# Memory projections first, the first feed-forward group split by token stream, and modulation weights on a second DMA queue

## The chip, the cores and the metric

The kernel runs on one core of one Trainium2 chip. The metric is the device time of one execution in microseconds, median over runs. The kernel before took 2076.3 us (three runs, 2075.75 to 2080.54).

## The reference, cut to what matters

Two transformer blocks follow each other on 512 latent tokens of width 1024, in float32. Only the first part of the first block is touched by the change:

```
cond_lat = silu(c);  cond_ctx = silu(c_ctx)
m_l = split(cond_lat @ ada_w + ada_b, 9)       # nine modulation vectors, latent tokens
m_c = split(cond_ctx @ ada_w + ada_b, 9)       # the same weights, context tokens
x   = x   + 0.5 * m_l[2] * swiglu(rms_norm(x,   norm1_w) * (1 + m_l[1]) + m_l[0], w1, w3, w2)
ctx = ctx + 0.5 * m_c[2] * swiglu(rms_norm(ctx, norm1_w) * (1 + m_c[1]) + m_c[0], w1, w3, w2)
...                                            # token mixing, a second swiglu
...                                            # second block; its cross attention needs
k = rms_norm(mem) @ w_ck;  v = rms_norm(mem) @ w_cv      # 256 memory tokens
```

x has 512 tokens, ctx and mem have 256 each. The inner width of swiglu is 2816, that is 22 tiles of 128 (f = 0 to 21). Both streams use the same w1, w3 and w2.

## The kernel before, in words

**Numbers.** Each float32 operand of a product is split in two parts of the matmul type, hi and lo. ScalarE makes hi, VectorE makes lo, and three matmuls (hi by hi, hi by lo, lo by hi) make one product. A unit of weights is a 128x1024 tile (512 KB): DMA into `wr`, ScalarE writes `wh`, VectorE writes `wl` (`wload`). A unit is 8 slices of depth, so 24 matmuls of 512 columns for x and 24 of 256 for ctx. `wspare` puts the two parts of a unit into slots of the general pool (`sh`, `sl`) in two halves of 512 columns.

**Buffers.** `wr` has 6 places and is shared by the weights of all products and by the modulation weights (`ada_w`); `wh` and `wl` have `WBUFS` = 5 places each.

**Modulation.** Each of the 9 modulation vectors is made of 8 tiles of `ada_w`, 512 KB each. VectorE multiplies a tile with `cond` and sums along the row, one instruction for each stream (output `junk`, result in a column of `mod`). `ada` does this for vectors 2 to 8, `ada_first` for vectors 0 and 1, inside `first_norm`, one depth slice k after the other.

**Queues.** Every DMA is issued by SyncE (SP), in one order. A load waits at the head of that queue until its place is free, and all loads behind it wait too.

**The planner.** The program writes operations in a program order into `Plan`. `issue()` then replays them with costs (`cost`, `HOPS`, a DMA of SP at 360 bytes a ns plus 50 ns, landing 2000 ns later) and fixes the order of each engine. When an engine is free, the planner takes, among the operations that could start about then, the oldest in program order; VectorE and ScalarE even wait a little for an older one (`YIELD`). On the chip each engine runs its list strictly in order.

**The order at the start.** `cond` and x are loaded, then mem; the first two of six steps of `memory()` come (steps 1 to 4 are one w_ck unit each, 5 and 6 a w_cv pair of units, and the results go to DRAM at the end). `first_norm(lat)` follows: the sum of squares of x, `rsqrt` (12 small VectorE operations), a broadcast (`rb`), and 8 slices k, each with two `ada_first` tiles, `xn`, `hh` and `hl`. As slices come, the first `FIRST` = 7 up-projection units run over them (`begin`), in 7 PSUM banks. Then come the other four steps of `memory()`, and the loads of ctx.

**The first feed-forward part.** `swiglu` takes the 22 tiles in four groups of 6, 6, 5 and 5. In a group, each f needs two up units (w1, w3), then `act` and the split `hi`, `lo`; after the group `project` adds the 8 down units (6 slices, 128x768, in the first group). In the first group (`ahead` = 6) the six f run for x alone, then the same six for ctx with the 12 units loaded again, then the down-projection takes both streams with one load of its weights. `ffn1_side(f)` inserts side steps after each f: two `first_norm(ctx_)` steps for f below 4, four `ada` steps for f = 4 and 5, and three from there on.

Of the kernel before, what the change touches and what calls it, by code (L numbers as in the profile page):

```python
# [11 lines left out]
F32 = mybir.dt.float32  # L12
F32R = mybir.dt.float32r
I32 = mybir.dt.int32
# [17 lines left out]
SLOTS = 60  # L32
WBUFS = 5
TAIL = 3
LEAD = 2

ALONE = 6
FIRST = 7

# [103 lines left out]
class Plan:  # L143
# [8 lines left out]
    PATIENCE = 6000  # L152
    YIELD = 0.3

    def __init__(self, tc):
        self.tc, self.ops, self.caps, self.warm = tc, [], {}, False

# [12 lines left out]
    def add(self, name, engine, method, args, kwargs):  # L170
        outs = [args[0]] + ([kwargs["accum_out"]] if "accum_out" in kwargs else [])
        outs = [x for x in outs if isinstance(x, View)]
        ins = [x for x in list(args[1:]) + [v for k, v in kwargs.items() if k != "accum_out"] if isinstance(x, View)]
        i = len(self.ops)
        deps = set()
        for x in ins:
            deps.update(x.tile.writer[p] for p in x.parts)
        for x in outs:
            for p in x.parts:
                deps.add(x.tile.writer[p])  # L180
                deps.update(x.tile.readers[p])
        for x in ins:
            for p in x.parts:
                x.tile.readers[p].append(i)
        for x in outs:
            for p in x.parts:
                x.tile.writer[p], x.tile.readers[p] = i, []
        deps.discard(None)
        deps.discard(i)
        tiles = {x.tile for x in ins + outs}  # L190
        for t in tiles:
            t.left += 1
            t.last = i
# [6 lines left out]
        self.ops.append((name, engine, method, args, kwargs, deps, tiles, cost, func))  # L200

    def cost(self, name, method, args, kwargs, outs, ins):
# [3 lines left out]
        if name == "PE":  # L206
# [25 lines left out]
    def issue(self):  # L232
# [50 lines left out]
        def pick(e):  # L283
# [26 lines left out]
        while oldest < n:  # L310
# [4 lines left out]
            t0, i = c  # L315
            name, engine, method, args, kwargs, deps, tiles, cost, func = ops[i]
            if func is not None and table not in func:
# [58 lines left out]
def tile_two_blocks(ctx: ExitStack, tc: tile.TileContext, a: dict, out: bass.AP, dbg=None):  # L376
# [128 lines left out]
    def rsqrt(m, cols):  # L505
        y = plan.tile(tp, [P, 32], F32, "rs_y", fresh("rsy"), 2)[:, :cols]
        t = plan.tile(tp, [P, 32], F32, "rs_t", fresh("rst"), 2)[:, :cols]
        V.tensor_scalar(y.bitcast(I32), m.bitcast(I32), 1, None, op0=ALU.logical_shift_right)
        V.tensor_scalar(y.bitcast(I32), y.bitcast(I32), -1, 0x5F3759DF, op0=ALU.mult, op1=ALU.add)
        for _ in range(3):  # L510
            V.tensor_mul(t, y, y)
            V.scalar_tensor_tensor(t, t, -0.5, m, op0=ALU.mult, op1=ALU.mult)
            V.scalar_tensor_tensor(y, t, 1.5, y, op0=ALU.add, op1=ALU.mult)
        return y

    def mean_eps(src, cols, scale):
        m = plan.tile(tp, [P, 32], F32, "rs_m", fresh("rsm"), 2)[:, :cols]
        V.tensor_scalar(m, src, scale, EPS, op0=ALU.mult, op1=ALU.add)
        return m
# [135 lines left out]
    def ada_first(c, s, k, junk):  # L655

        w = wraw(a["ada_w"][c, k], 1024)
        V.tensor_tensor_reduce(junk, w, cond[s], 1.0, col("ada_b", NK * c + k), ALU.mult, ALU.add,
# [106 lines left out]

# [43 lines left out]

    def swiglu(streams, up, down, groups, gate, side=None, after=None, each=None, begun=(), ahead=0):  # L810


        f0, first = 0, ahead
        for g, F in enumerate(groups):
            hid = {st: [] for st in streams}

# [6 lines left out]
            def some(f, part):  # L823
# [10 lines left out]
                ws = [None if ps[i] else wcols(wload(up[2 * f + i])) for i in range(2)]  # L834
                if g == 0 and f < LEAD and not first:
                    for span in spans_of(streams):
# [24 lines left out]
            project(lambda o: wcols(wload(down[g][o], F * P), F), lambda st: hid[st], update, streams,  # L861
                    after if g == len(groups) - 1 else None, each if g == len(groups) - 1 else None)
            f0 += F

    normal = first_norm(ctx_)
    rest = (step for c in range(2, 9) for step in ada(c, (0, 1) if c < 5 else (0,)))

    def ffn1_side(f):
        if f < 4:
            for _ in range(2):  # L870
                next(normal, None)
        else:
            for _ in range(4 if f < 6 else 3):
                next(rest, None)

    swiglu([lat, ctx_], a["ffn1_up"], [a[f"ffn1_dn{g}"] for g in range(len(FFN1_GROUPS))], FFN1_GROUPS,
           per_stream(lambda s: half_gate(2, s)), ffn1_side,
           renorm(per_stream(lambda s: gain_of("norm2_w", 4, s)), per_stream(lambda s: shift_of(3, s))), begun=sums, ahead=ALONE)
    for k in range(NK):
# [872 lines left out]
```

## Time and profile before

| | us |
|---|---|
| median of three runs | 2076.3 |
| profiled execution, its own time | 2077.35 |
| its span, first to last instruction | 2075.5 |
| TensorE busy | 2009.8 |
| VectorE busy | 1190.4 |
| ScalarE busy | 794.5 |

The profiled execution lies 1.05 us over the median and inside the range of the runs. TensorE is busy for 97% of the span, but its busy time also counts matmuls at half clock. PE is TensorE, DVE VectorE, ACT ScalarE, POOL GpSimd and SP SyncE.

### The profile page before, as it was taken

What the parts mean: (1) busy time and instruction counts of PE and PEld (TensorE: products, weight loads), DVE (VectorE), ACT (ScalarE), POOL (GpSimd) and SP (SyncE); (2) the same over time, 40 slices, a digit from 0 to 9 for tenths busy, and PEclk for the clock granted to TensorE, in tenths of its full rate; (3) what the DMA queues carried; (4) which work ended last, traced back from release to release, by engine and by line L of the source; (5) the groups of instructions that cost most, each with busy time, mean ns of one, the idle gap of its engine ahead of it and who ended that gap; (6) DMA issues with size and microseconds to landing.
All of it is one profiled execution on the core that took longest, in us unless ns stands there. A gap on an engine that the chain in (4) does not pass through costs nothing.

```text
span 2075.5 us, 27876 instructions
## 1 busy us (share of the span) xinstructions
PE 2009.8 (97%) x11033; PEld 1688.6 (81%) x11033; DVE 1190.4 (57%) x2157; ACT 794.5 (38%) x1238; POOL 121.1 (6%) x126
## 2 busy tenths in 40 slices
PE   5889999999999998999999999999998999999998
PEld 4779888888888876978988888888765888888887
DVE  7887844426247788589633333374866655343344
ACT  5452121221225654374432222343676363233231
POOL 0000000000000023110000000001243010000000
PEclk9989999999999999999999999999997999999999
DMA  8866624417132112232233323234321214333321
GB/s 312 270 236 199 196 77 140 145 60 224 51 107 94 45 52 72 67 91 83 71 117 101 97 92 104 86 94 124 85 74 27 64 59 132 101 92 102 93 70 41
DMA packets 73538, 225.57 MB, mean 109 GB/s; under 512 B 9360, under 2 KB 12096, under 8 KB 73408
## 3 DMA queue, kind: packets, MB, share of 16 engines
q1 hardware_dynamic: 73408, 223.80, 34.7%
q8 instruction: 86, 1.41, 0.3%
q14 instruction: 44, 0.36, 0.1%
HBM read 210.00 MB, written 5.24 MB: 104 GB/s over the span
## 4 chain that ended last, share of the span: by engine, by line
PE 87%; issue 5%; DVE 3%; DMA 2%; ACT 2%; POOL 1%; SPq 0%; DVEq 0%; ACTq 0%; POOLq 0%
PE p L363 77%; PE as L363 1%; PE gs L363 1%; PE ro L363 1%; PE rs L363 1%; PE at L363 1%; PE ao L363 1%; PE st L363 1%; PE go L363 1%; DVE junk L363 1%; DMA wr<-in_ffn_up_dram 1%; PE gl L363 1%; DVE rg_r L363 0%; PE rb L363 0%; POOL pg L363 0%
## 5 line engine op out<-in xcount | busy, mean ns | idle before, releaser
L363 ACT ACTIVATE wh<-wr 128x1024 fp32r<-128x1024 f32 (+4 forms) x295 | 298.2, 1012 | 751.1 <-PE p L363 566.1
L363 PE MATMUL p<-hh,wh 128*128 128x512 f32 (+1 forms) x1320 | 505.2, 389 | 13.2 <-ACT hh L363 7.9
L363 PE MATMUL p<-hl,wh 128*128 128x512 f32 (+1 forms) x1320 | 507.2, 388 | 0.0
L363 DVE TENSOR_TENSOR wl<-wr,wh 128x1024 fp32r<-128x1024 f32 (+4 forms) x295 | 345.9, 1177 | 170.7 <-ACT wh L363 77.6
L363 PE MATMUL p<-hh,wl 128*128 128x512 f32 (+1 forms) x1320 | 363.4, 387 | 4.3 <-DVE wl L363 4.3
L363 PE MATMUL p<-lo,wh 128*128 128x512 f32 (+1 forms) x831 | 310.0, 381 | 2.5 <-DVE lo L363 2.5
L363 PE MATMUL p<-hi,wh 128*128 128x512 f32 (+1 forms) x831 | 308.7, 380 | 2.0 <-ACT hi L363 2.0
L363 PEld LDWEIGHTS p<-hh,wh 128*128 128x128 f32 x1320 | 248.9, 190 | 57.6 <-ACT hh L363 10.4
L363 PEld LDWEIGHTS p<-hh,wl 128*128 128x128 f32 x1320 | 243.9, 190 | 54.5 <-DVE wl L363 4.7
L363 PEld LDWEIGHTS p<-hl,wh 128*128 128x128 f32 x1320 | 250.9, 191 | 37.5 <-issue 1.3
L363 PE MATMUL p<-hi,wl 128*128 128x512 f32 (+1 forms) x831 | 211.6, 375 | 0.0
L363 PEld LDWEIGHTS p<-lo,wh 128*128 128x128 f32 x831 | 158.6, 191 | 27.4 <-DVE lo L363 3.2
L363 PEld LDWEIGHTS p<-hi,wh 128*128 128x128 f32 x831 | 158.3, 191 | 24.4 <-ACT hi L363 2.2
L363 PEld LDWEIGHTS p<-hi,wl 128*128 128x128 f32 x831 | 148.8, 188 | 27.2
L363 PEld LDWEIGHTS p<-h,wh 128*128 128x128 f32 x816 | 138.8, 189 | 26.1
L363 DVE CUSTOM_DVE_ANT_0 junk<-wr,cond,vec 128x1024 f32<-128x1024 f32 x112 | 143.3, 1281 | 21.0 <-DMA wr<-in_ada_w_dram 20.1
L363 PE MATMUL p<-h,wh 128*128 128x256 f32 x816 | 145.5, 280 | 0.0
L363 DVE TENSOR_TENSOR act<-act,p 128x512 f32<-128x512 f32 (+1 forms) x68 | 38.3, 583 | 176.9 <-PE p L363 175.5
L363 DVE SCALAR_TENSOR_TENSOR x<-p,gate,x 128x512 f32<-128x512 f32 (+1 forms) x59 | 42.6, 723 | 106.0 <-PE p L363 106.0
L363 DVE TENSOR_TENSOR x<-p,x 128x512 f32<-128x512 f32 (+1 forms) x51 | 33.6, 658 | 112.9 <-PE p L363 112.7
L363 PE MATMUL p<-h,wl 128*128 128x256 f32 x408 | 97.3, 279 | 0.0
L363 PEld LDWEIGHTS p<-hid,wh 128*128 128x128 f32 x352 | 64.3, 188 | 14.3
(344 smaller groups left out, 2434.6 us busy)
## 6 DMA issues: line engine op xcount, KB each, us to landing
wr<-in_ffn_up_dram SPq DMA_DIRECT2D x100, 512.0 KB, 3.7
wr<-in_ada_w_dram SPq DMA_DIRECT2D x88, 512.0 KB, 4.4
wr<-in_mlp_up_dram SPq DMA_DIRECT2D x32, 512.0 KB, 3.6
wr<-in_mlp_dn_dram SPq DMA_DIRECT2D x32, 512.0 KB, 3.6
wr<-in_w_out_dram SPq DMA_DIRECT2D x16, 512.0 KB, 4.2
wr<-in_ffn_dn_dram SPq DMA_DIRECT2D x16, 448.0 KB, 3.2
wr<-in_ffn_dn_dram SPq DMA_DIRECT2D x16, 384.0 KB, 3.2
wr<-in_ffn_dn_dram SPq DMA_DIRECT2D x16, 320.0 KB, 2.8
```

The source lines that it names most:

```text
L363: ins = getattr(engine, method)(*args, **kwargs).ins
```

## The change

The memory stream is loaded ahead of x, the first memory step runs ahead of `first_norm(lat)`, and one more memory step follows after each slice. `cond` is loaded after x. The number of units begun early is 6. The first group runs whole for x, down-projection included, then whole for ctx; both its up and its down weights are loaded twice. Three side steps follow each f of each pass; they are now vector 2 for x (8 steps), the load and the first norm of ctx (8), vector 2 for ctx (8), then vectors 3 to 8. The modulation weights get 3 places of their own (`wa`) and are issued by GpSimd; `wr` has 5 places, `wh` and `wl` have 4. The planner treats a DMA of any queue by the cost of SP's, and VectorE takes an operation of `mean_eps` and `rsqrt` ahead of older ones if it can start within 200 ns.

```
-WBUFS = 5
+WBUFS = 4
+RAWS = 5
+ARAWS = 3
...
-ALONE = 6
-FIRST = 7
+FIRST = 6
...
+    RUSH = 200
+    LANDING = 2000
+    def hurry(self):          # a context in which self.urgent is True
...
-        if name == "SP":
+        if method == "dma_start":
             x = outs[0] if outs else ins[0]
             return int(np.prod(x.shape)) * 4 / 360.0 + 50
...
             if e in ("DVE", "ACT"):
+                rush = [c for c in cand if ops[c[1]][9] and c[0] - first <= self.RUSH]
+                if rush:
+                    return min(rush)
...
-            landed = end + (2000 if e == "SP" else 0)
+            landed = end + (self.LANDING if method == "dma_start" else 0)
...
-    def wraw(ap, cols):
-        raw = plan.tile(wp, [P, 1024], F32, "wr", fresh("wr"), 6)
-        sync.dma_start(raw[:, :cols], ap)
+    def wraw(ap, cols, queue=sync, tag="wr", n=RAWS):
+        raw = plan.tile(wp, [P, 1024], F32, tag, fresh(tag), n)
+        queue.dma_start(raw[:, :cols], ap)
         return raw
+
+    def araw(c, j):
+        return wraw(a["ada_w"][c, j], 1024, G, "wa", ARAWS)
...                            # rsqrt and mean_eps: the same operations, inside "with plan.hurry():"
-            w = wraw(a["ada_w"][c, j], 1024)
+            w = araw(c, j)
...                            # the same in ada_first
-    cond = [conditions(0), None]
+    mem = load(NC, "mem", a["memT"])
+    early = memory()
+    next(early)
     lat = load(NL, "x", a["xT"])
     xt = lat.x
-    mem = load(NC, "mem", a["memT"])
-    early = memory()
-    for _ in range(2):
-        next(early)
+    cond = [conditions(0), None]
...
     for k in range(NK):
         next(normal)
+        next(early, None)
...
-    for _ in early:
-        pass
-    ctx_ = load(NC, "ctx", a["ctxT"])
-    cond[1] = conditions(1)
+    ctx_ = Stream(NC, None)
...
-        f0, first = 0, ahead
-        for g, F in enumerate(groups):
-            hid = {st: [] for st in streams}
+        passes = [(0, [st]) for st in streams] if apart else [(0, streams)]
+        passes += [(g, streams) for g in range(1, len(groups))]
+        count = 0
+        for g, part in passes:
+            f0, F = sum(groups[:g]), groups[g]
+            hid = {st: [] for st in part}
...
-                some(f, streams[:1] if f < first else streams)
-                if f == first - 1:
-                    for e in range(first):
-                        some(e, streams[1:])
+                some(f, part)
                 if side is not None:
-                    side(f)
+                    side(count)
+                count += 1
...                            # project(...) takes part instead of streams
+    def second_norm():
+        ctx_.x = load(NC, "ctx", a["ctxT"]).x
+        cond[1] = conditions(1)
+        yield from first_norm(ctx_)
...
+    rest = chain(ada(2, (0,)), second_norm(), ada(2, (1,)),
+                 *(ada(c, (0, 1) if c < 5 else (0,)) for c in range(3, 9)))
+
+    def ffn1_side(i):
+        for _ in range(3):
+            next(rest, None)
```

## Rows read from the trace of the kernel before

**Rows 1.** The page: busy time of each engine, share of the span, instructions.
```profile
PE 2009.8 (97%) x11033; PEld 1688.6 (81%) x11033; DVE 1190.4 (57%) x2157; ACT 794.5 (38%) x1238; POOL 121.1 (6%) x126
```

**Rows 2.** Windows by stage: length, then busy us and instructions of each engine.
```profile
core 0: us, PE busy (x) PEld busy (x) DVE busy (x) ACT busy (x) POOL busy (x), PEclk, DMA share, GB/s
0.00:79.20 79.20, 57.67 (x253) 47.26 (x254) 61.65 (x131) 45.14 (x77) 0.70 (x6) 0.94 0.85 296
79.20:126.80 47.60, 36.40 (x212) 31.84 (x211) 40.20 (x86) 20.08 (x34) 0.00 (x0) 0.86 0.76 243
126.80:226.90 100.10, 100.10 (x643) 90.70 (x642) 81.71 (x123) 32.96 (x43) 0.00 (x0) 1.00 0.67 214
...
600.00:900.00 300.00, 287.94 (x2161) 244.09 (x2160) 213.97 (x440) 146.63 (x266) 48.15 (x56) 0.99 0.24 73
...
1450.00:1700.00 250.00, 239.04 (x1199) 176.44 (x1198) 168.72 (x322) 147.30 (x269) 66.41 (x60) 0.93 0.21 59
1700.00:2075.50 375.50, 365.55 (x1701) 306.19 (x1699) 168.28 (x247) 121.82 (x158) 0.00 (x0) 0.99 0.30 91
```

**Rows 3.** Waits of PE, 0 to 126.8 us: total, times, longest.
```profile
PE st L363 <- DVE ss L363: 13.3, 1, 13.3
PE p L363 <- ACT hh L363: 6.7, 5, 3.8
PE p L363 <- ACT wh L363: 5.3, 3, 2.3
PE p L363 <- DVE wl L363: 4.3, 1, 4.3
PE rb L363 <- DVE rsy L363: 2.9, 1, 2.9
```

**Rows 4.** Timeline of SP's queue: start, length, count, in the first 112 us.
```profile
1.63 4.63 SPq L363 DMA_DIRECT2D x<-in_xT_dram  x8
7.23 2.35 SPq L363 DMA_DIRECT2D mem<-in_memT_dram  x4
...
97.92 12.78 SPq L363 DMA_DIRECT2D wr<-in_ada_w_dram  x4
111.98 1.84 SPq L363 DMA_DIRECT2D wr<-in_ffn_up_dram  x2
```

**Rows 5.** Timeline, ACT and PE: the unit that was loaded late.
```profile
117.22 1.06 ACT L363 ACTIVATE wh<-wr 128x1024 fp32r<-128x1024 f32 x1 [3.67 <-DMA wr<-in_ffn_up_dram]
...
118.33 0.80 PE L363 MATMUL p<-hh,wh 128*128 128x512 f32 x1 [1.80 <-ACT wh L363]
```

**Rows 6.** Timeline of PE at full clock: spacing of matmuls, 512 and 256 columns.
```profile
69.67 0.39 PE L363 MATMUL p<-hh,wh 128*128 128x512 f32 x1
...
78.97 0.39 PE L363 MATMUL p<-hh,sl 128*128 128x512 f32 x1
...
82.07 2.08 PE L363 MATMUL p<-h,sh 128*128 128x256 f32 x16
83.98 1.12 PE L363 MATMUL p<-h,sl 128*128 128x256 f32 x8
```

**Rows 7.** Groups of DVE by form, 0 to 226.9: busy us, mean ns, idle before.
```profile
L363 DVE CUSTOM_DVE_ANT_0 junk<-wr,cond,vec 128x1024 f32<-128x1024 f32 x64 | 81.9, 1280 | 3.9 <-DMA wr<-in_ada_w_dram 3.3
L363 DVE TENSOR_TENSOR wl<-wr,wh 128x1024 fp32r<-128x1024 f32 x26 | 31.1, 1218 | 0.0
L363 DVE TENSOR_TENSOR sl<-wr,sh 128x512 fp32r<-128x512 f32 x20 | 13.3, 688 | 1.6 <-PE p L363 1.0 <-issue 0.5
L363 DVE TENSOR_TENSOR wl<-wr,wh 128x768 fp32r<-128x768 f32 x8 | 7.4, 949 | 0.0
```

**Rows 8.** Timeline of DVE: first and last operation of x's reciprocal root (merged with mem's).
```profile
16.95 0.16 DVE L363 TENSOR_SCALAR rsm<-st 128x4 f32<-128x4 f32 x1 [0.49 <-PE st L363]
...
25.74 0.23 DVE L363 SCALAR_TENSOR_TENSOR rsy<-rst,rsy 128x2 f32<-128x2 f32 x2
```

**Rows 9.** DMA issues: count, KB each, median us to landing; the page, then 10:80.
```profile
wr<-in_ada_w_dram SPq DMA_DIRECT2D x88, 512.0 KB, 4.4
...
wr<-in_ada_w_dram SPq DMA_DIRECT2D x20, 512.0 KB, 5.4
```

More of the change, by code (lines that the diff above doesn't have):

```diff
@@ L153, with __enter__, __exit__ @@
     YIELD = 0.3
+    RUSH = 200
+    LANDING = 2000
     def __init__(self, tc):
-        self.tc, self.ops, self.caps, self.warm = tc, [], {}, False
+        self.tc, self.ops, self.caps, self.warm, self.urgent = tc, [], {}, False, False
+    def hurry(self):
+        plan = self
+        class Hurry:
+            def __enter__(self):
+                plan.urgent = True
+            def __exit__(self, *_):
+                plan.urgent = False
+        return Hurry()
     def engine(self, name, engine):
@@ L199, in add @@
         cost = self.cost(name, method, args, kwargs, outs, ins)
-        self.ops.append((name, engine, method, args, kwargs, deps, tiles, cost, func))
+        self.ops.append((name, engine, method, args, kwargs, deps, tiles, cost, func, self.urgent))
     def cost(self, name, method, args, kwargs, outs, ins):
@@ L315, in issue @@
             t0, i = c
-            name, engine, method, args, kwargs, deps, tiles, cost, func = ops[i]
+            name, engine, method, args, kwargs, deps, tiles, cost, func, _ = ops[i]
             if func is not None and table not in func:
@@ L507, in rsqrt @@
         t = plan.tile(tp, [P, 32], F32, "rs_t", fresh("rst"), 2)[:, :cols]
[L508 to L513, printed above, removed]
+        with plan.hurry():
+            V.tensor_scalar(y.bitcast(I32), m.bitcast(I32), 1, None, op0=ALU.logical_shift_right)
+            V.tensor_scalar(y.bitcast(I32), y.bitcast(I32), -1, 0x5F3759DF, op0=ALU.mult, op1=ALU.add)
+            for _ in range(3):
+                V.tensor_mul(t, y, y)
+                V.scalar_tensor_tensor(t, t, -0.5, m, op0=ALU.mult, op1=ALU.mult)
+                V.scalar_tensor_tensor(y, t, 1.5, y, op0=ALU.add, op1=ALU.mult)
         return y
@@ L517, in mean_eps @@
         m = plan.tile(tp, [P, 32], F32, "rs_m", fresh("rsm"), 2)[:, :cols]
-        V.tensor_scalar(m, src, scale, EPS, op0=ALU.mult, op1=ALU.add)
+        with plan.hurry():
+            V.tensor_scalar(m, src, scale, EPS, op0=ALU.mult, op1=ALU.add)
         return m
@@ L655, in ada_first @@
     def ada_first(c, s, k, junk):
-        w = wraw(a["ada_w"][c, k], 1024)
+        w = araw(c, k)
         V.tensor_tensor_reduce(junk, w, cond[s], 1.0, col("ada_b", NK * c + k), ALU.mult, ALU.add,
@@ L807, in log1p_exp_neg, with swiglu @@
         return s
-    def swiglu(streams, up, down, groups, gate, side=None, after=None, each=None, begun=(), ahead=0):
-        f0, first = 0, ahead
-        for g, F in enumerate(groups):
-            hid = {st: [] for st in streams}
+    def swiglu(streams, up, down, groups, gate, side=None, after=None, each=None, begun=(), apart=False):
+        passes = [(0, [st]) for st in streams] if apart else [(0, streams)]
[4 more added lines that the diff above has]
+            hid = {st: [] for st in part}
             def finish(span, t, hi, lo, p1, p3):
@@ L834, in some @@
                 ws = [None if ps[i] else wcols(wload(up[2 * f + i])) for i in range(2)]
-                if g == 0 and f < LEAD and not first:
+                if g == 0 and f < LEAD and not apart:
                     for span in spans_of(streams):
@@ L859, in update, with chain @@
                 V.scalar_tensor_tensor(st.x[o][:, x:y], po, gate(st)(o), st.x[o][:, x:y], op0=ALU.mult, op1=ALU.add)
-            project(lambda o: wcols(wload(down[g][o], F * P), F), lambda st: hid[st], update, streams,
+            project(lambda o: wcols(wload(down[g][o], F * P), F), lambda st: hid[st], update, part,
                     after if g == len(groups) - 1 else None, each if g == len(groups) - 1 else None)
[L863 to L874, printed above, removed]
+    def second_norm():
+        ctx_.x = load(NC, "ctx", a["ctxT"]).x
+        cond[1] = conditions(1)
+        yield from first_norm(ctx_)
+    def chain(*steps):
+        for s in steps:
+            yield from s
+    rest = chain(ada(2, (0,)), second_norm(), ada(2, (1,)),
+                 *(ada(c, (0, 1) if c < 5 else (0,)) for c in range(3, 9)))
+    def ffn1_side(i):
+        for _ in range(3):
+            next(rest, None)
     swiglu([lat, ctx_], a["ffn1_up"], [a[f"ffn1_dn{g}"] for g in range(len(FFN1_GROUPS))], FFN1_GROUPS,
            per_stream(lambda s: half_gate(2, s)), ffn1_side,
-           renorm(per_stream(lambda s: gain_of("norm2_w", 4, s)), per_stream(lambda s: shift_of(3, s))), begun=sums, ahead=ALONE)
+           renorm(per_stream(lambda s: gain_of("norm2_w", 4, s)), per_stream(lambda s: shift_of(3, s))), begun=sums, apart=True)
     for k in range(NK):
```

## The prediction

> **What bounds the kernel now.** I read the page's busy times first. PE is busy 2009.8 of 2075.5 us [rows 1], so 65.7 us of idle time and whatever the half clock costs is all that can be won. The windows by stage say where they lie [rows 2]: 21.5 us up to 79.2, 11.2 us from there to 126.8, none up to 900 except 12.1 us after 600, and some 21 us in the last two rows. The change edits only the start; the later stages keep their work, so I look at the first 226.9 us, the time at which the first feed-forward group ends.
>
> Idle time is not all that is lost there, since the granted clock is 0.94 and 0.86 in the first two stretches against 1.00 in the third. I count work instead. At full clock 41 matmuls of 512 columns take 9.30 us, 0.227 each, and 16 of 256 columns 1.91 us, 0.119 each [rows 6]. By the code the 253 matmuls of the first stretch are 7 units x 24 = 168 wide ones, 48 of 256 columns (two memory units) and some 36 small ones (0.12 taken for each): 38.1 + 5.7 + 4.3 = 48.1 us of work in 79.2 us, so 31.1 us are lost. The 212 of the second are 144 of memory, 12 small ones and 56 wide: 17.1 + 1.4 + 12.7 = 31.2 us of work, 16.4 us lost. Together 47.5 us are lost, and the whole first group with all that stands ahead of it is 226.9 - 47.5 = 179.4 us of PE work.
>
> The waits name the causes [rows 3]. The 13.3 us are the first bytes: x, then the sum of squares. The ACT hh waits are the slices of x's first norm. The ACT wh and DVE wl waits are units that came late. For those see SP's queue: four modulation loads stand at its head for 12.78 us from 97.92, and the next up units go out at 111.98 [rows 4]. One of them is split at 117.22 and PE restarts at 118.33 [rows 5]. So the loss of the second stretch comes from one shared ring and one shared queue, with VectorE behind them: it frees a place only after its `junk` instruction.
>
> And VectorE is nearly full itself: 61.65 + 40.20 + 81.71 = 183.6 busy us of 226.9 [rows 2], with 64 junks at 1.28 us as the largest item [rows 7].
>
> **The change part by part.**
>
> *Memory first.* x's first DMA goes out at 1.63 us now [rows 4]. Ahead of it come 1 MB of mem and 0.5 MB of w_ck, while 1.5 MB of modulation tiles run on the other queue; at the 296 GB/s of the first row [rows 2] 1.5 to 3 MB are 5 to 10 us. x's statistics are that much later, but PE has a memory unit to do, and the chain of the reciprocal root, 16.95 to 25.97 us now with other work between its 12 operations [rows 8], can run in 12 x 0.2 = 2.4 us once `hurry` puts them first. The two cancel within a few us, and I take nothing for the start of the slices. What counts is that all eight memory units (4 w_ck, 2 pairs of w_cv, 192 matmuls) now fill holes between slices. At the end of the early sums PE has done 144 x 0.227 + 192 x 0.119 + 36 x 0.12 = 59.8 us of work. The slices are set by VectorE, which gets 9 more half-unit splits there at 0.69 us [rows 7] and loses a junk and the seventh unit's split, 2.5 us: +3.7 us. If half of this is hidden in VectorE's own holes, the sums end at 81, and 21 us are lost in place of 31.1: -10.
>
> *Own ring and own queue.* Up units no longer wait behind modulation tiles, and ctx's norm runs beside x's remaining three f and its down-projection, 6 x 24 x 0.227 + 8 x 18 x 0.227 = 65.4 us of PE work. The 16.4 us of the second stretch go. With the term above, PE alone would end the group at 179.4 + 21 = 200.4.
>
> *What VectorE then has to do.* Eight down units of the first group are split once more, 8 x 0.949 = 7.6 us [rows 7]. The side steps now follow 12 passes over f and not 6: by program order 72 junks (16 of x's norm, 8, 16 of ctx's norm, 8, 16, 8) are older than the end of the group, against 64 now: 8 x 1.36 with the read of the sum = 10.9 us. (Vector 2 costs 8 more loads, no more junks: two single ones in place of a pair.) VectorE's work to the end of the group is 183.6 + 7.6 + 10.9 = 202.1 us. Its idle time was 43.3 us. It cannot start before the first bytes, so at least 8 us remain; I take 15, and 25 as the other end. Half of the last side step, some 4 us, may trail behind. That puts the end at 202 + 15 - 4 = 213, between 202 and 227: VectorE, not PE, sets it. The loss comes back in the ctx pass, where an f is 48 x 0.119 = 5.7 us of PE work, but two splits (2.4 us), three steps with up to six junks (8.2 us) and more for VectorE; the planner gives it the oldest first, and that is the junk of the f before, while the unit that PE wants next waits behind it.
>
> *Three places for modulation tiles.* A tile's place turns round in 5.2 us in the planner (0.13 + 1.51 + 2.0 + 0.13 + 1.4). In the trace the load alone takes 4.4 us, and 5.4 where DMA is busy [rows 9], so 6.1 to 7.1 with issue and junk. Where single junks follow each other (32 tiles behind x's norm, 10.7 turns) VectorE can stand 0.9 to 1.9 us a turn, 10 to 20 us in all, if nothing else were planned between; in most turns something is, so 0 to 20 with 4 taken, for this and for a low clock behind the holes. No row shows a DMA issued by GpSimd; I take the landing of SP's for it, from 4.4 us to 5.4 and 2.5 more for the range. The Trainium skill, DMA: Bandwidth & Descriptors, Specifications, gives the GpSimd path a first byte after about 1 us against 0.6 on SP's path; 0.4 us on 10.7 turns would be 4 us, and the sum would be 2071 by it, an estimate. No row here shows it.
>
> *The rest at nothing.* One place less for `wr`, `wh` and `wl` still leaves four units, over 20 us of PE work at 24 x 0.227 = 5.4 us a unit, against some 7 us for load and split; if that cover is gone it shows in the windows from 600 on, 3 us either way. `hurry` later in the kernel moves operations of 0.16 us under a busy PE. The 8 added down loads and 8 added modulation loads, 7 MB, fit into a DMA share of 0.67 to 0.85.
>
> **The sum.** The group ends at 213 + 4 = 217 in place of 226.9: -9.9. From the profiled execution, 2077.35 us, that is 2067.4; it lies 1.05 us over the median, inside the spread of the runs, and I give **2067**. About 0.3%, 6.2 us, is what a measurement of this kernel can tell from no change.
>
> **The rivals.**
>
> *VectorE lags without harm (0.18).* A junk whose tile has not come lets a split go first, so the backlog slides into the next group, where an f of both streams is 16.6 us of PE work. Then PE alone sets the end, 200 to 204: 2050 to 2055. For it: two-thirds of the turns above have a hole for one split. Against it: vectors 3 and 4 have two junks a tile, 2.7 us, and no hole.
>
> *Loss moved, not removed (0.24).* VectorE idles 25 us as it waits for x, cond and late tiles, and the ctx pass starves: end at 221 to 232, 2071 to 2082. For it: VectorE was 0.78 busy in the first stretch even with full rings.
>
> *Modulation tiles land late (0.25).* The order of VectorE is fixed by a planner that believes in 2.0 us and in two queues that do not share bandwidth. If a tile takes 2.5 us more than 4.4, every turn holds the splits behind it: 10.7 x 2.5 = 27 us more, end at 244, 2094. It decides against the change from about 5.9 us of landing on (1.5 x 10.7 = 16 us). For it: 5.4 us already in 10:80 with one queue. Against it: x's slices leave 8 us for three junks. The Trainium skill, SBUF — State Buffer, section SBUF: two separate sides, has a mechanism for it: GpSimd cannot write descriptors while VectorE runs in a two-port mode. The large groups of rows 7 are two-input operations, which by that page hold off only GpSimd operations that read SBUF, so by the rule little is to be feared.
>
> **Chances.** The forecast's own case, 2060 to 2070, has 0.33. Faster by over 0.3%: 0.33 + 0.18 = 0.51. Within: 0.24. Slower: 0.25. The range from 2049 to 2092 takes in the PE-bound case below and most of the late tiles above, and leaves some 0.18 outside.
>
> **What would show it.** In the profile of after: PE's first matmul near 10 us; the sums done near 81; no wait of SP for `mod` ahead of an up load; PE idle in the ctx pass on ACT wh or DVE wl with VectorE at 0.9 or more; the step to continuous 512-and-256 pairs near 217. Wrong if VectorE is below 0.85 in that stretch, if junk waits for DMA exceed 20 us, or if the stages from 600 on move by more than 5 us.

## The result and the profile after

The changed kernel takes 2106.2 us (median of 4 runs, 2099.8 to 2108.3) against 2078.4 beside it (4 runs, 2075.8 to 2081.3): a ratio of 1.0122, 95% interval 1.0094 to 1.0151. A second set of four runs gave 1.0118 (1.0089 to 1.0147). It is slower by 1.2%; 2067 was predicted, and the range ended at 2092. The profiled execution took 2104.78 us, its span is 2103.0, 27.5 more than before.

The page of the changed kernel shows PE 11 us busier, and DVE only by 10 (columns as in [rows 1]):

```profile
PE 2020.9 (96%) x11033; PEld 1696.6 (81%) x11033; DVE 1200.1 (57%) x2165; ACT 803.3 (38%) x1247; POOL 172.9 (8%) x222
```

PE does the same instructions as before; 11 us more of busy time is a lower granted clock (0.976 over the span against 0.981), the other 16 of the 27.5 are idle time. The windows by stage of the changed kernel say where (columns as in [rows 2]; the third window ends where the second group begins, 246.20 here and 226.76 before):

```profile
0.00:79.20 79.20, 54.91 (x307) 48.70 (x308) 57.83 (x121) 44.00 (x78) 9.30 (x22) 0.91 0.88 310
79.20:126.80 47.60, 43.26 (x193) 35.33 (x193) 41.37 (x83) 19.45 (x28) 10.03 (x19) 0.98 0.73 229
126.80:246.20 119.40, 100.78 (x608) 91.16 (x606) 101.25 (x158) 39.93 (x54) 14.77 (x28) 0.91 0.74 247
...
1700.00:2103.00 403.00, 392.31 (x1859) 328.86 (x1857) 182.59 (x291) 140.64 (x211) 7.38 (x13) 0.99 0.28 88
```

The third stretch was full in before, at clock 1.00 [rows 2]; now PE idles 18.6 us in it, at 0.91. With the 179.4 us of PE work that the prediction counted, 246.2 - 179.4 = 66.8 us are lost up to there in place of 47.4: 19.4 of the 27.5 us lie in the first group. DVE is busy 57.83 + 41.37 + 101.25 = 200.5 us in it and idle for 45.7: 21.4 us up to 79.2, 6.2 from there to 126.8, and 18.1 behind. What PE waited for there, 0 to 246.2 us (total, times, longest):

```profile
PE p L383 <- DVE wl L383: 21.5, 6, 7.0
PE p L383 <- ACT sh L383: 17.2, 3, 13.3
PE rb L383 <- DVE rsy L383: 2.5, 1, 2.5
PE st L383 <- DVE ss L383: 2.2, 1, 2.2
```

The ACT hh and ACT wh waits of [rows 3] have almost gone; DVE wl, a unit whose low half is not split, has become the largest. The timeline of PE shows these holes: two in the passes of the latent tokens, two in those of the context, and the second group's first matmul at the end.

```profile
125.60 5.40 PE L383 MATMUL p<-hh,wl 128*128 128x512 f32 x16 [4.12 <-DVE wl L383]
142.52 5.45 PE L383 MATMUL p<-hh,wl 128*128 128x512 f32 x16 [6.97 <-DVE wl L383]
...
219.31 2.08 PE L383 MATMUL p<-h,wl 128*128 128x256 f32 x8 [4.44 <-DVE wl L383]
231.93 1.65 PE L383 MATMUL p<-hid,wl 128*128 128x256 f32 x6 [4.38 <-DVE wl L383]
...
246.20 0.40 PE L383 MATMUL p<-hh,wh 128*128 128x512 f32 x1
```

And this is VectorE ahead of the hole at 219.31:

```profile
211.09 0.42 DVE L383 TENSOR_TENSOR act<-act,p 128x256 f32<-128x256 f32 x1 [0.41 <-PE p L383]
211.43 1.28 DVE L383 CUSTOM_DVE_ANT_0 junk<-wa,cond,vec 128x1024 f32<-128x1024 f32 x1
...
212.64 0.42 DVE L383 TENSOR_TENSOR hid<-act,hid 128x256 fp32r<-128x256 f32 x1
212.98 1.28 DVE L383 CUSTOM_DVE_ANT_0 junk<-wa,cond,vec 128x1024 f32<-128x1024 f32 x1
...
214.30 1.28 DVE L383 CUSTOM_DVE_ANT_0 junk<-wa,cond,vec 128x1024 f32<-128x1024 f32 x1
...
215.51 1.28 DVE L383 CUSTOM_DVE_ANT_0 junk<-wa,cond,vec 128x1024 f32<-128x1024 f32 x1
...
216.83 1.28 DVE L383 CUSTOM_DVE_ANT_0 junk<-wa,cond,vec 128x1024 f32<-128x1024 f32 x1
...
218.04 2.36 DVE L383 TENSOR_TENSOR wl<-wr,wh 128x1024 fp32r<-128x1024 f32 x2
220.31 1.28 DVE L383 CUSTOM_DVE_ANT_0 junk<-wa,cond,vec 128x1024 f32<-128x1024 f32 x1
...
223.85 0.42 DVE L383 TENSOR_TENSOR act<-act,p 128x256 f32<-128x256 f32 x1 [2.25 <-PE p L383]
```

Five junks run with one short operation between them, none waits for its tile, and only then come the two splits. PE, idle for 4.44 us, starts when the first of them is done, and then VectorE waits 2.25 us for PE's result. The two engines take turns. Of VectorE's 18.1 idle us behind 126.8, its waits for PE make up 12.7 us; the two largest are:

```profile
DVE act L383 <- PE p L383: 10.0, 7, 2.3
DVE ctx L383 <- PE p L383: 2.4, 3, 1.4
```

ScalarE stands behind the same splits, since wh and wl have four places each:

```profile
219.34 0.84 ACT L383 ACTIVATE wh<-wr 128x768 fp32r<-128x768 f32 x1 [6.09 <-DVE wl L383]
```

The start is late as well. The eight slices of x's norm, by DVE's operation on tile xn (first and last start), ran from 29.9 to 69.1 in before; in the changed kernel:

```profile
L383 DVE TENSOR_TENSOR xn<-x,rbs x8: 684/687/693, 34.2 to 83.2; 128x512 f32<-128x512 f32 x8
```

That is 4.3 us later, and 7.0 us a slice in place of 5.6. The early sums end at 94.0.

### The profile page after: what moved, and what is told of

The parts are those of the page before. It is cut to its first block, busy times and chain, and to the rows that moved or that the text cites. A ratio compares the mean times of both kernels' runs of the same rounds, so it can differ in the third digit from the quotient of the medians.

```text
span 2103.0 us, 27943 instructions
## 1 busy us (share of the span) xinstructions
PE 2020.9 (96%) x11033; PEld 1696.6 (81%) x11033; DVE 1200.1 (57%) x2165; ACT 803.3 (38%) x1247; POOL 172.9 (8%) x222
## 4 chain that ended last, share of the span: by engine, by line
PE 84%; issue 5%; DVE 5%; DMA 2%; ACT 2%; POOL 1%; SPq 0%; DVEq 0%; POOLq 0%; ACTq 0%
PE p L383 75%; PE as L383 1%; PE gs L383 1%; DMA wr<-in_ffn_up_dram 1%; PE ro L383 1%; PE st L383 1%; DVE junk L383 1%; PE rs L383 1%; PE go L383 1%; PE at L383 1%; PE ao L383 1%; PE gl L383 1%; PE rb L383 0%; DMA wr<-in_w_ck_dram 0%; DMA wa<-in_ada_w_dram 0%
## 5 line engine op out<-in xcount | busy, mean ns | idle before, releaser
L383 ACT ACTIVATE wh<-wr 128x1024 fp32r<-128x1024 f32 (+4 forms) x303 | 305.0, 1008 | 731.2 <-PE p L383 521.6
L383 DVE TENSOR_TENSOR wl<-wr,wh 128x1024 fp32r<-128x1024 f32 (+4 forms) x303 | 355.0, 1175 | 158.9 <-ACT wh L383 78.9
L383 PE MATMUL p<-hi,wl 128*128 128x512 f32 (+1 forms) x831 | 206.1, 374 | 0.0
L383 PEld LDWEIGHTS p<-hi,wl 128*128 128x128 f32 x831 | 148.7, 188 | 27.5 <-DVE wl L383 0.3
L383 DVE CUSTOM_DVE_ANT_0 junk<-wa,cond,vec 128x1024 f32<-128x1024 f32 x112 | 143.1, 1281 | 13.5 <-DMA wa<-in_ada_w_dram 12.1
L383 PEld LDWEIGHTS p<-h,wl 128*128 128x128 f32 x408 | 71.2, 194 | 6.3 <-DVE wl L383 6.2
```

The lines of the kernel that those rows point to most:

```text
L383: ins = getattr(engine, method)(*args, **kwargs).ins
```

## The experiments

Sixteen runs followed, e15 and e16 of the two kernels themselves. Of each are given the ratio to before with its 95% interval; the **group end**, the first matmul of the second group in the trace (226.8 in before, 246.2 in the changed kernel); and, where it helps, the **time at equal clock**: span times mean granted clock over 0.981, the mean over the runs. Spans of before lie up to 19 us apart, and with them the mean clock (0.976 to 0.987); their product lies between 2072 and 2082 in single runs, and its mean hardly moves. In four sets of 24 to 31 runs before comes to 2076.4, 2076.9, 2076.8 and 2076.6. PE's work being the same, this number follows PE's idle time: 65.7 us over the whole span in before, and 82.1 in the changed kernel, which comes to 2094.2. The group end is that of one profile each; two profiles of before put it at 226.8 and 224.1, so a difference below 3 us in it says little.

**Does VectorE's order starve PE, or its amount of work?** e1 takes steps out of the context's pass, e2 changes the order alone: it marks the splits of the first group's units with `hurry`, so that the planner gives them ahead of older operations.

```diff
 def ffn1_side(i):
-    for _ in range(3):
+    for _ in range(1 if 6 <= i < 12 else 3):
         next(rest, None)
```

> The changed kernel with one modulation step instead of three behind each of the six f of the context pass; the 12 steps left out there follow in the later groups, so nothing is left out of the computation. Theory A (VectorE works off modulation tiles that are older in the program than the splits TensorE waits for): 24 junks x 1.36 = 33 us of VectorE work leave a pass that took some 71 us for 51 us of TensorE work; the context pass loses most of its 20 us, the first group ends at 228 to 235 instead of 247, and the time is 2087 to 2094. Theory B (the up and down units themselves come late over the DMA, VectorE only waits with them): within 3 us of the changed kernel's 2106. Theory C (the junks only move their stall into the next group): the first group ends earlier, but the stage up to 670 gives it back and the time stays above 2100.

Measured: 1.0033 (1.0008 to 1.0057), group end 230.5. Both numbers of A came, 2089.3 us being 17 less than the changed kernel. B and C fall: the junks cost little where they went (2080.8 at equal clock against 2094.2).

```diff
+    def rushed(ap, cols):      # wload, for the first group's units
+        ...
+        with plan.hurry():
+            split(hi[:, :cols], lo[:, :cols], raw[:, :cols])
```

> The changed kernel, with the splits of the first group's up and down units marked like the reciprocal root, so that the planner gives them ahead of older junks; the work is the same. Theory A (order): TensorE gets its units in time, the junks slide behind; the first group ends at 230 to 237, 2089 to 2096. Theory D (amount: VectorE has too much to do before the group's end, whatever the order, since the outputs of an f need it too): gain below 4 us, 2102 to 2108.

Measured: 1.0011 (0.9983 to 1.0040), 2081.9 us, group end 227.3. With the same work in another order the first group ends 18.9 us earlier, and in the median the loss against before is no longer measurable; at equal clock (2080.9) some 4.5 us of it are left. That is more than A expected; D falls. Not all of the 18.9 us is idle time won: up to its group end VectorE is busy 187.7 us here, 12.8 less than in the changed kernel, and idle for 39.6, 6.1 less. e6 marks the outputs of each f too.

```diff
+                with plan.hurry() if apart and g == 0 else ExitStack():
                     S_.activation(t[:, x:y], p1, AF.Silu)
                     V.tensor_mul(t[:, x:y], t[:, x:y], p3)
                     split(hi, lo, t[:, x:y])
```

> As e2_split_first, and the three output operations of each f of the first group marked too, so that every junk yields to what TensorE waits for. In e2 one wait of 10.2 us for an output (hi) was left in the latent pass. Theory A: that wait goes and the first group ends 6 to 10 us earlier than e2's 227.3, at 217 to 221; the time 2070 to 2078, 4 to 10 us below e2. Theory D (the wait only moves, to the gate's tiles or to context's norm, which the junks feed): the group ends within 3 us of 227.3 and the time stays within 4 us of e2.

Measured: 1.0026 (1.0004 to 1.0049), group end 217.2. The end is as A expected, the median is not: it is 2080.1, within 4 us of e2, as D had it. At equal clock e6 comes to 2076.6, 4.3 below e2, so part of what the group won is there. In the two profiles the rest took 1857.7 us in e6 and 1849.6 in e2, which is for the most part the clock (see e15). VectorE in the context's pass of e6:

```profile
182.95 0.42 DVE L383 TENSOR_TENSOR act<-act,p 128x256 f32<-128x256 f32 x1 [0.34 <-PE p L383]
183.29 1.22 DVE L383 TENSOR_TENSOR wl<-wr,wh 128x1024 fp32r<-128x1024 f32 x1
184.43 0.42 DVE L383 TENSOR_TENSOR hid<-act,hid 128x256 fp32r<-128x256 f32 x1
184.76 1.28 DVE L383 CUSTOM_DVE_ANT_0 junk<-wa,cond,vec 128x1024 f32<-128x1024 f32 x1
...
185.97 1.22 DVE L383 TENSOR_TENSOR wl<-wr,wh 128x1024 fp32r<-128x1024 f32 x1
187.11 1.28 DVE L383 CUSTOM_DVE_ANT_0 junk<-wa,cond,vec 128x1024 f32<-128x1024 f32 x1
```

One junk stands between two splits, not five. Up to the group's end VectorE is busy 178.2 us here against 200.5: the junks that nobody waits for slide into the next groups (58 start before the end, 72 in the changed kernel). The windows up to the group end, e2 and then e6 (columns as in [rows 2]):

```profile
0.00:227.33 227.33, 189.58 (x1104) 168.32 (x1105) 187.69 (x340) 103.49 (x161) 32.24 (x66) 0.95 0.81 277
0.00:217.24 217.24, 188.52 (x1104) 168.35 (x1105) 178.22 (x326) 104.19 (x161) 30.02 (x61) 0.97 0.83 281
```

**The start.** e3 gives the head the order of before; e7 gives SP the tiles of x's norm as well; e8 does two memory units ahead of the slices and six behind them.

```diff
+    cond = [conditions(0), None]
+    lat = load(NL, "x", a["xT"])
     mem = load(NC, "mem", a["memT"])
     early = memory()
     next(early)
-    lat = load(NL, "x", a["xT"])
-    cond = [conditions(0), None]
```

> The changed kernel with the three loads at its head in the order of the kernel before: conditions, x, then memory. Theory S (x and the conditions stand behind 1.5 MB of memory and the modulation tiles, and every slice of x's norm is late by that): x's reciprocal root ends near 20 instead of 29.7, the sums end at 82 to 87 instead of 93, and the time is 6 to 11 us less, 2095 to 2100. Theory T (the slices are set by VectorE's amount of work with the memory splits, not by their start): the sums end within 3 us of 93 and the time stays within 3 us of 2106.

Measured: 1.0126 (1.0090 to 1.0162), group end 246.2, slices from 35.8 to 84.1. T, the slices starting even later than without the edit. The order at the head is worth nothing while a second queue loads tiles beside it. From issue to landing, in the first 42 us (count, KB each, median us), before:

```profile
x<-in_xT_dram SPq DMA_DIRECT2D x8, 256.0 KB, 6.1
```

and the changed kernel:

```profile
wa<-in_ada_w_dram POOLq DMA_DIRECT2D x7, 512.0 KB, 5.7
x<-in_xT_dram SPq DMA_DIRECT2D x8, 256.0 KB, 9.0
```

The Trainium skill, DMA: Bandwidth & Descriptors, Rules for kernel authors, says that issuing from several engines wins no bandwidth, since all run on the same 16 DMA engines and interleave. The trace agrees: x's pieces take half as long again (9.6 us in e3, where they go out first) while tiles land beside them of which the changed kernel uses none before 24 us.

```diff
-        w = araw(c, k)
+        w = wraw(a["ada_w"][c, k], 1024, sync if s == 0 else G, "wa", ARAWS)
```

> As e6_outputs_too, with conditions and x loaded first as in the kernel before, and the modulation tiles of x's own norm issued by SP behind x (own ring kept); all later tiles stay with GpSimd. Theory Q (with a second queue 1.5 MB of tiles land beside x from the first microsecond and take its bandwidth: x's loads took 9.6 to 10.3 us against 6.1, whichever order stood at the head): x's first slice starts near 30 instead of 35 and the time is 3 to 7 us below e6. Rival T (the slices are paced by VectorE and ScalarE work, not by their start): the last slice stays within 2 us of 85, and the time within 2 us of e6.

Measured: 1.0036 (1.0014 to 1.0058), group end 224.1, first slice at 36.5. The edit does not test Q. GpSimd's queue still sends three tiles, of later vectors now, at the very start:

```profile
1.29 0.72 POOL L383 DMA_DIRECT2D wa<-in_ada_w_dram  x1 [0.35 <-issue]
...
2.35 1.09 POOL L383 DMA_DIRECT2D wa<-in_ada_w_dram  x2
```

So 1.5 MB land beside x as before, and x's loads still took 9.6 us. T falls: the last slice starts at 65.0, 18.6 us earlier than in e6, and yet the group ends 6.8 us later and the median is 5.7 us longer. PE's first matmul came at 20.9 us (13.8 in e6); whether that is the reason no run shows.

```diff
     early = memory()
-    next(early)
+    for _ in range(2):
+        next(early)
 ...
         next(normal)
-        next(early, None)
 ...
+    for _ in early:
+        pass
     ctx_ = Stream(NC, None)
```

> As e6_outputs_too, with two memory units ahead of the slices and the other six behind them, as in the kernel before. Theory M (the nine half-unit splits between the slices stretch them from 5.6 to 7.1 us each): the slices end near 74 instead of 85; what is won there is spent on the memory units behind, which TensorE then has in one piece, so the group ends between 4 us earlier and 6 us later than in e6. Theory P (the memory units fill holes that are there anyway): the group ends 6 to 12 us later and the time is as much above e6.

Measured: 1.0001 (0.9978 to 1.0023), group end 217.0, slices in e8:

```profile
L383 DVE TENSOR_TENSOR xn<-x,rbs x8: 685/689/693, 36.3 to 73.0; 128x512 f32<-128x512 f32 x8
```

5.2 us a slice in place of 7.0, and the same end: M, near its middle. The memory units stretch the slices as much as they save behind them, so "memory first" is worth nothing at the group end in either direction (2074.4 at equal clock, 2 us below e6).

**Ring and queue.** e4 puts only the own ring and GpSimd's queue into before. e10 takes both out of the changed kernel. e12 and e13 do the same with the marks of e6 and the memory order of e8: own ring on SP's queue, and shared ring.

```diff
-WBUFS = 5
+WBUFS = 4
...
-        raw = plan.tile(wp, [P, 1024], F32, "wr", fresh("wr"), 6)
+    def araw(c, j):
+        return wraw(a["ada_w"][c, j], 1024, G, "wa", 3)      # other loads: "wr", 5
```

> The kernel before with only the own ring and GpSimd's queue for modulation tiles, and the one place less for each of the three unit rings that pays for it; the order of the first group and of its start stays. As the prediction put it (the shared ring and queue cost 16.4 us between 79.2 and 126.8): 8 to 16 us less than before's 2078, 2062 to 2070. Rival R2 (tiles on that queue land late, with VectorE's fixed order behind them): 2085 to 2095. Rival V (VectorE takes the place of the ring: the same junks stand ahead of the same splits): within 5 us of 2078.

Measured: 1.0031 (1.0010 to 1.0051), 2084.1 us, group end 232.1. The queue and ring that were to win 16 us lose 5 at the group end, and 11 at equal clock (2087.8). V names part of it: PE's idle time from 79.2 to 126.8 falls from 11.2 to 3.1 us, as the prediction had it, and 9.2 us of it come behind, where before had none. The time lies 1 us beyond V's range, since the start is worse as well: x's pieces took 10.3 us to land, the first slice began at 38.9, and PE idled 30.0 us up to 79.2 in place of 21.5. R2 is out: behind the first tile, junks waited 3.6 us for their tiles.

```diff
-        return wraw(a["ada_w"][c, j], 1024, G, "wa", ARAWS)
+        return wraw(a["ada_w"][c, j], 1024)
```

(and the places of before, 6 raw and 5 split)

> The changed kernel with modulation tiles back on SP's queue and in the shared ring, and the places of before (6 raw, 5 split); memory first, the first group apart, the three steps an f and the marks on the root stay. Theory A (the loss is made by VectorE's order, whatever the queue): the first group ends at 238 to 250, the time is 2092 to 2106. Theory Q (the second queue, or the places given up for it, makes the loss): the group ends at 220 to 230, 2068 to 2082.

Measured: 1.0073 (1.0045 to 1.0101), group end 240.0. A by the end, its time missed by 1 us: without own ring and queue the loss stays, though smaller (2087.3 at equal clock).

```diff
-        return wraw(a["ada_w"][c, j], 1024, G, "wa", ARAWS)
+        return wraw(a["ada_w"][c, j], 1024, sync, "wa", ARAWS)
```

> As e8_memory_last, with the tiles issued by SP again but in their own ring of three. Theory Q2 (own queue: a tile that waits for its place no longer holds the units behind it on SP): without it the first group ends at 222 to 232 instead of 217, and the time is 5 to 15 us above e8. Rival N (the ring is what matters, or nothing does): the group ends within 3 us of 217 and the time within 4 us of e8.

Measured: 0.9961 (0.9940 to 0.9982), 2068.1 us, group end 212.8. Both theories fall: taking GpSimd's queue away is a gain, 4.2 us of the group (the ratio's interval just overlaps that of e8). x's pieces land in 7.7 us (9.7 in e8), the first slice starts at 33.7 (36.3), and PE idles 20.7 us up to 79.2 (25.1), so the gain lies at the start. This version beats both kernels.

e13 has e10's edit on top of e8's kernel, with e10's places.

> As e12_tiles_on_sp, but with the shared ring and the places of before (6 raw, 5 split): what is left of the change is the first group apart, the context's norm beside it and the marks. Ring theory (tiles and units that share six places hold each other up even when VectorE gives the units first): the first group ends at 218 to 228 instead of 212.8, and span times clock over 0.981 is 2074 or more, against 2068.3 for e12. Rival (one queue, in the right order, is enough): within 3 us of e12 in both.

Measured: 1.0059 (1.0036 to 1.0083), group end 237.6, 2082.4 at equal clock. The ring theory, and more: 24.8 us. SP's queue in e13 shows it (start, length, count):

```profile
94.64 10.90 SPq L383 DMA_DIRECT2D wr<-in_ada_w_dram  x6
106.75 4.95 SPq L383 DMA_DIRECT2D wr<-in_ffn_up_dram  x2
116.64 7.99 SPq L383 DMA_DIRECT2D wr<-in_ada_w_dram  x6
125.84 4.69 SPq L383 DMA_DIRECT2D wr<-in_ffn_up_dram  x2
```

Six tiles stand ahead of two units, and six again ahead of the next two; the longest of PE's waits in e13 but the first is one of 5.4 us for ACT wh. With the own ring (e12) one to three tiles go out between units:

```profile
117.55 2.13 SPq L383 DMA_DIRECT2D wa<-in_ada_w_dram  x2
120.28 0.33 SPq L383 DMA_DIRECT2D wr<-in_ffn_dn_dram  x1
121.82 2.12 SPq L383 DMA_DIRECT2D wa<-in_ada_w_dram  x2
```

e14 has e3's edit on top of e12.

> As e12_tiles_on_sp, with the conditions and x ahead of memory in SP's queue, as in the kernel before. Theory S2 (with one queue the order at the head counts again, which two queues had hidden in e3): x's first slice starts near 30 instead of 33.7 and the group ends 2 to 4 us earlier, near 210; span times clock over 0.981 near 2065. Rival T2 (TensorE loses at the start, with no memory unit to do, what it wins in the slices): within 2 us of 212.8 and of 2068.3.

Measured: 0.9962 (0.9943 to 0.9981), group end 215.2, first slice at 32.4, 2072.9 at equal clock. S2 falls, T2 is missed to the worse side, by 0.4 us of group end and 2.6 of time: also with one queue the order at the head wins nothing.

**The marks on before.** e11 adds to before the two kinds of marks of e6 (with the planner's few lines for them) and nothing else:

```diff
-                ws = [None if ps[i] else wcols(wload(up[2 * f + i])) for i in range(2)]
+                ws = [None if ps[i] else wcols(rushed(up[2 * f + i], 1024)) if ahead and g == 0 else wcols(wload(up[2 * f + i])) for i in range(2)]
```

> The kernel before with nothing but the marks: the splits and the outputs of its first group go ahead of older junks. Theory A (the order is what both kernels lose by): the first group ends at 215 to 222 instead of 227.5 and the time is 5 to 10 us below before. Rival V (in before the units themselves come late, behind four tiles in SP's queue): the group ends at 225 to 230 and the time is within 4 us of before.

Measured: 1.0012 (0.9986 to 1.0038), group end 225.6: V. In before the units themselves come late, behind tiles in SP's queue [rows 4]; PE still waited 8.5 us for ACT wh from 79 on.

**The stages behind the first group.** e5 is before with four split places and five raw ones; e9 is e8 with five split places, paid by one raw and one tile place; e15 and e16 are the two kernels again.

```diff
-WBUFS = 5
+WBUFS = 4
...
-        raw = plan.tile(wp, [P, 1024], F32, "wr", fresh("wr"), 6)
+        raw = plan.tile(wp, [P, 1024], F32, "wr", fresh("wr"), 5)
```

> The kernel before with only one place less in each of the three unit rings (five raw units, four split ones); tiles stay on SP's queue in the shared ring. Theory W (the places cost time in the later stages: from the gate matmuls of the token mixing to the statistics of its heads the changed kernel took 285.2 us against 278.5, and all five kernels with four places took 285 to 289): the same stretch takes 284 to 288 here, and the time is 5 to 9 us above before. Rival (the stretch is longer by the clock alone, after gaps that fall otherwise): 278 to 281 there, and within 4 us of before.

Measured: 1.0035 (1.0011 to 1.0059), 2083.1 us against 2076.5; group end 228.3; the stretch took 292.2 us, longer than even W had it, and the median fits W as well. But at equal clock the kernel comes to 2078.0, 1.1 over before beside it: what is longer is the clock, and whether the places make a low clock likelier is not shown.

```diff
-WBUFS = 4
-RAWS = 5
-ARAWS = 3
+WBUFS = 5
+RAWS = 4
+ARAWS = 2
```

> As e8_memory_last, with five places again for split units, paid by one raw place and one tile place (4 raw, 2 tiles). Theory W (the fourth split place is what the later stages miss): from the gate matmuls to the head statistics 278 to 281 us instead of 285 to 294, the first group still ends near 217, and the time is 2066 to 2072, faster than before. Rival R (two tile places and four raw ones are too few in the first group): the group ends at 225 or later and the time is 2075 or more. Rival L (the clock in that stretch falls by where its short gaps lie, and not by the places): the stretch stays at 283 or more.

Measured: 1.0068 (1.0038 to 1.0098); group end 224.3, the stretch 293.5. W falls, L holds, and so does R but for 0.7 us of the end: five split places didn't shorten the stretch, and four raw and two tile places lengthened the first group.

> The kernel before, unchanged, for a second profile. Theory K (the clock in the token mixing differs from execution to execution of one program): mean clock between 0.976 and 0.987 over the runs, and span times clock over 0.981 within 2 us of 2076.8 in every one; the stretch from the gate matmuls to the head statistics (278.5 us in the first profile) may be 278 to 290. Theory C (that stretch is steady in one program, and longer only in changed ones): 278 to 280.

Measured: 1.0005 (0.9985 to 1.0025); group end 224.1, the stretch 282.7, mean clock 0.977 to 0.985. K for the stretch and the clock; at equal clock single runs spread from 2074.0 to 2081.8, more than the 2 us I gave.

> The changed kernel, unchanged, for more runs. Theory K: span times clock over 0.981 stays at 2092 to 2097 in every run, 16 to 20 us above before, and the mean clock varies by 0.006 or more between runs, so that 17 us of the loss are the program's and the rest is the clock's. Theory C: mean clock below 0.979 in every run, since the program itself makes the holes that lower it.

Measured: 2102.0 us, 1.0118 (1.0089 to 1.0147); group end 246.6; at equal clock 2091.4 (2094.2 in the first set), 15 to 18 over before, single runs at 2087.8 to 2093.5 and so partly below K's range. The mean clock lay at 0.974 to 0.978, which fits C better than K; in the first set one run had 0.980. With four runs each I leave that open.

How much the clock does is seen in one place of the token mixing, some 79 us behind the first gate matmul. Before (columns as in [rows 2]):

```profile
749.60:800.00 50.40, 47.75 (x400) 33.51 (x400) 36.14 (x76) 28.18 (x50) 11.97 (x20) 1.00 0.21 53
```

the same program once more, in e15:

```profile
746.90:797.30 50.40, 47.73 (x359) 32.36 (x358) 33.03 (x69) 26.62 (x47) 11.97 (x20) 0.93 0.17 48
```

and in e8:

```profile
743.00:793.00 50.00, 47.78 (x296) 31.84 (x296) 25.67 (x56) 20.72 (x39) 11.95 (x20) 0.80 0.14 37
```

PE is busy 47.7 to 47.8 us in all three and idle for 2.2 to 2.7, and does 400, 359 and 296 instructions.

## Why the prediction was wrong

**The step that failed is VectorE's idle time.** The prediction had VectorE set the end by its work, 202.1 us, plus 15 us of idle time (8 to 25, though its lower end of 202 leaves out even the 8). The work was right: 200.5 us, with the 72 junks that were counted. The idle time is 246.2 - 200.5 = 45.7, about what it was in before (43.3). Of the 37.4 us between the forecast's 2067.4 and the profiled 2104.8, 29.2 lie in the group end, and this term, 30.7 too small, makes them up. The 15 had no reason but the first bytes; up to 126.8 alone it is 27.6 us, which no run took apart, and 18.1 come behind. For these the mechanism was written down (oldest first, the junk ahead of the split), as a reason for the sum, without being priced: every unit held behind junks stops PE, and a stopped PE then leaves VectorE without a result to work on, 12.7 us of waits for PE. The prediction looked for this in the context's pass; the two holes of PE in the latent passes are as long, 4.12 + 6.97 us against 4.44 + 4.38.

e2 and e6 show what the order costs PE, with the same operations: 18.9 us of group end, and 10.1 more. But VectorE's idle time is the smaller part of that: in e6 it is 217.2 - 178.2 = 39.0, 6.7 less, while 22.3 us of VectorE's work slide behind the end. No kernel here came below 34.9 (e12). So the frame of the sum, VectorE's work plus its idle time, holds only while all older work must run ahead of the end. The forecast's 217 is what the changed kernel reaches once PE's operations go first, by luck and not by the forecast's path.

**Own ring: right cause, wrong partner.** The 16.4 us were put down to the shared ring and queue, and were to go with them. In the second stretch they did: PE's idle time there went from 11.2 to 4.3 us. But it came back behind. The four combinations of ring and order, all with the first group apart, tell it (group end; time at equal clock): shared ring and oldest first 240.0; 2087.3 (e10), own ring alone 246.2; 2094.2 (the change), marks alone 237.6; 2082.4 (e13), both 217.0; 2074.4 (e8, with GpSimd's queue as in the change) or 212.8; 2068.3 (e12, on SP's queue). (The two with marks have e8's memory order, which e8 showed to be worth nothing at the group end.) The own ring alone moves the end 6 us up. The marks alone move it 2 down, which two profiles of one kernel can differ by; at equal clock it is 5. Both together move it 23 to 27 down (13 to 19 at equal clock). An own ring on SP's queue with the oldest first was not run, so the 6 us hold the price of the second queue as well. With the ring freed, VectorE's order sets the pace; with the order mended, the shared ring does. The change removed one of two limits that lay behind each other.

**The second queue is a cost.** It was costed at the landing of a tile alone. The tiles came on time: 4.7 us median over all 96 (4.4 in [rows 9]), and junks waited for them 2.6 us up to the group's end. So rival R2, late tiles, is out. The trap that the Trainium skill describes on SBUF — State Buffer, section SBUF: two separate sides (a GpSimd load whose descriptors wait while VectorE runs in a two-port mode) did not show, as the prediction had it. But the tiles land beside x at the start. The price is 4.2 us of group end (e8 to e12); at equal clock 2074.4 and 2068.3.

**Memory first.** The sums were to end at 81 and ended at 94.0. The slices started 4.3 us late, which I had set off against the faster chain of the root; and each took 1.4 us more, where I had hidden half of VectorE's 3.7 us. But this term was no part of the loss: e8 gives 10 us of it back at the slices and ends at the same place. It had been credited with 10 us of gain, in the end that PE alone would set (200.4) and not in the sum, and is worth nothing. The sign given for it, PE's first matmul near 10 us, was missed too: it came at 13.27, the 13.3 us of the second row of waits.

**Rivals.** R3, the loss moved and not removed, named what happened, VectorE idle and the context's passes starved, at 221 to 232. It had the size wrong by 14 us: its 25 us of idle time are about what lies ahead of 126.8 (27.6), and the waits for PE behind that are not in it. The sign of VectorE at 0.9 in the context's passes was missed: from 126.8 on it was busy 101.25 of 119.4 us, 0.848, just on the side that the prediction named as wrong. That SP no longer waits for mod ahead of an up load was right.

**The rest at nothing.** From the group end on before took 1848.7 and 1852.6 us, the changed kernel 1856.8 and 1853.4, and all eighteen profiles lie between 1848 and 1862 whatever their places. PE's idle time in it is 33.0 and 34.8 us before, 34.8 and 35.7 after. So some 2 us may be the places; the rest of the 8 us between the two first profiles, more than the 5 us that the prediction named as a sign against it, is the clock. Whether the changed kernel draws the lower clock more often than before, or its runs did by chance, stays open.

## What to carry to other kernels

Where one engine serves both urgent and patient work in a fixed order, the sum of its work does not bound the time: look for what the other engine waits for and what stands ahead of it in that queue, price one full turn of mutual waiting, and ask which of the work may slide behind the end. An idle time read from a trace stays in the sum until a reason takes it out. When two limits lie behind each other, removing one shows little, and a single-edit test of either will call it harmless; try both together before discarding one. Here the second DMA queue cost time beside an urgent load, and it was better to keep the order in one queue and give the patient loads a ring of their own.

## What the runs showed of the hardware

Loads issued by GpSimd landed nearly as fast as SP's (4.7 us against 4.4 for 512 KB), at 0.53 us of its time each. The mean granted clock of one unchanged program lay anywhere between 0.976 and 0.987 from run to run, which is most of the 19 us by which its spans differ; a single profile can be off by that. In the same place of the same program, with 2.7 us of idle time both times, PE was granted 1.00 in one execution and 0.93 in another, and e8 had 0.80 there.
